# Bias tables from sixteen row copies, read in eighths, and a residual's copy through DRAM issued between weight loads

## The chip, the cores and the metric

The kernel runs on one core of a Trainium2 chip. The metric is the device time of one execution in microseconds (us); a kernel's time is the median of its runs.

## The reference, cut to what matters

A decoder trunk of two layers on 256 tokens of width 1024, all in float32. Each layer adds half a SwiGLU feed-forward, then a mixer, then half a second feed-forward (FFN). Layer 0 mixes with a diagonal state space model (S5); layer 1 with attention whose keys and values are computed once, after layer 0.

```
for layer in range(2):
    h = h + 0.5 * swiglu(rmsnorm(h), w_in (1024 x 5632), w_out (2816 x 1024))
    h = h + mixer(rmsnorm(h))            # layer 0: S5, layer 1: attention
    h = h + 0.5 * swiglu(rmsnorm(h), ...)
    if layer == 0: kv = shared_kv(h)
# attention: logits = q.k * scale + rel_bias[bucket(t - s)], masked where t < s
```

The attention bias depends only on the distance of query and key, for 16 heads: a table of 16 x 256 numbers, which the kernel lays out once as a tile B, with one shifted row per query.

## The kernel before

**Products.** TensorE (PE) has each product in three passes (`mm3`, lines 124 to 126): activations and weights are split into a high and a low half, and high x high, high x low, low x high are added up. Weights come from DRAM as granules of 1 MB (`load_granule`, line 76, issued by SP, two buffers `raw`). ScalarE (ACT) makes the high half, VectorE (DVE) the low half (lines 105 and 108 where a norm's gain is applied, else 92 and 96), half a granule at a time, into five buffers `whi` and five `wlo`.

**An FFN** (`ffn`) goes through 11 chunks of 256 hidden columns. Chunk c first has 48 matmuls of the input product (two granules, tiles `mm`), then SiLU and gate on ACT and DVE (lines 256, 257, tile `g`), then the 24 matmuls of the output product of chunk c-1 (one granule, tiles `o`, in `second`). The transposes of `g` of chunk c-1 on PE (line 211, `transposed`) and their split into the tile `turned` (lines 149 ACT, 150 DVE) stand after the fifth of the chunk's eight k steps. For the last chunk nothing follows: all of `second` of chunk 9, then the four transposes of chunk 10, then `second` of chunk 10, which ends the FFN with the residual added to h (line 235). There are four FFNs; in the second (`w_in2_0`) `perm` is set, and the split of `turned` takes two operations on each engine.

**Work beside the products** is given to `ffn` as a generator `bg`. `background(bg, steps)` is called after each odd k step and at the end of a chunk (once in chunk 0, five times in each later one) and advances the generator; a `yield n` costs n of the calls (a bare `yield` one). What it traces is put behind the last weight split (ACT, DVE) and the last weight load (SP) traced before it.

**The order on each queue** is set when the kernel is built: instructions are taken in traced order, each when the builder's own clock says that what it needs is there, so later loads can go ahead of an earlier copy that is not ready. Each queue then runs in that order on the chip and waits at each instruction for its inputs.

**Around the second FFN.** S5 leaves h with its tokens permuted. Ahead of the FFN, h is written to a DRAM tile `hd` by four copies (line 1019) and read back in natural order by two (line 1021), all issued by SP; `kv_consts` loads small constants; then the FFN runs with `bias_tables` as its background. That multiplies the bias by a one-hot table (line 647, two matmuls), copies the result to `rev` (128 partitions x 384: head h in partition h, repeated eight times), and GpSimd (POOL) issues eight copies `revd<-rev` (line 654), each of 16 partitions, each row sixteen times; then one read `B<-revd` of 2 MB (line 659), 128 partitions. B is first read in the attention, some 410 us later.

Of the kernel before, what the change touches and what calls it, by code (L numbers as in the profile page):

```python
# [9 lines left out]
F32 = mybir.dt.float32  # L10
# [6 lines left out]
P = 128  # L17
D = 1024
# [3 lines left out]
NCH = FF // 256  # L22
# [10 lines left out]
def kernel(ctx: ExitStack, tc: tile.TileContext, A, out):  # L33
    nc = tc.nc
# [9 lines left out]
    dscr = ctx.enter_context(tc.tile_pool(name="dscr", bufs=1, space=bass.MemoryType.DRAM))  # L44
# [4 lines left out]
    def mm_bank():  # L49
        return Banks.mm.tile([P, 512], F32, name="mm")  # L50

    def tr_bank():
        return Banks.tr.tile([P, 512], F32, name=Banks.tag)

    def turn_room():

        return low.tile([P, 2, 1024], F32R, name="turned")


    h = pers.tile([P, 2, D], F32, name="h")  # L60
# [52 lines left out]
    def granules(aps, w=512, gain=None, first=(), eng="av"):  # L113
        for n, ap in enumerate(aps):
            raw = first[n] if n < len(first) else load_granule(ap, w)
            for j in range(2):
                hi, lo = split_half(raw, j, w, gain, ((n % 2) * 2 + j) * 2, eng)
                for s_ in range(2):
                    yield hi[:, s_ * w:(s_ + 1) * w], lo[:, s_ * w:(s_ + 1) * w]
# [77 lines left out]
    def ffn(x, gi, w_in, w_out, res, perm=False, bg=None, steps=1, done=None, first=()):  # L197
        with tc.tile_pool(name="ffn", bufs=2) as fp, tc.tile_pool(name="ps_a", bufs=1, space=PSUM) as pa:
            xT, rs = x.xT, x.rs
            gTs = turn_room()  # L200
            acc2 = [[pa.tile([P, 512], F32, name=f"o{t}{hf}") for hf in range(2)] for t in range(2)]
            g_in = granules([w_in[c, kh] for c in range(NCH) for kh in range(2)], gain=gi, first=first)
            g_out = granules([w_out[j] for j in range(NCH)])

            def transposed(c, g):

                gT = gTs[:, c % 2].rearrange("p (i f c) -> p i f c", i=2, f=2)
                ps = tr_bank()
                for f in range(2):
                    for t in range(2):  # L210
                        T.transpose(ps[:, (f * 2 + t) * P:(f * 2 + t + 1) * P], g[:, t, f * P:(f + 1) * P], ident)  # L211
                if perm:
                    src = ps.rearrange("p (f t e c) -> p f t e c", f=2, t=2, e=2)
                    hi, lo = (gT[:, i].rearrange("p f (c t e) -> p f t e c", t=2, e=2) for i in range(2))
                    for f in range(2):
                        split(hi[:, f], lo[:, f], src[:, f])
                else:
                    split(gT[:, 0], gT[:, 1], ps.rearrange("p (f c) -> p f c", f=2))
                return gT

            def second(c, gT):
                if c < NCH - 1:
                    for f in range(2):
                        for hf in range(2):
                            w = next(g_out)
                            for t in range(2):
                                mm3(acc2[t][hf], gT, f, t, w, c + f == 0, False)
                    return
                ws = [[next(g_out) for _ in range(2)] for _ in range(2)]
                for t in range(2):  # L230
                    for hf in range(2):
                        for f in range(2):
                            mm3(acc2[t][hf], gT, f, t, ws[f][hf], False, f == 1)
                        cs = slice(hf * 512, (hf + 1) * 512)
                        V.scalar_tensor_tensor(out=res[:, t, cs], in0=acc2[t][hf], scalar=0.5, in1=res[:, t, cs], op0=ALU.mult, op1=ALU.add)
                        done(t, hf)

            prev = None
            for c in range(NCH):
                acc = [mm_bank() for _ in range(2)]  # L240
                gT = None
                if c == 0:
                    gemm(acc, xT, g_in, lead=True)
                else:
                    for k in range(KT):
                        w = next(g_in)
                        for t in range(2):
                            mm3(acc[t], xT, k, t, w, k == 0, k == KT - 1)
                        if k == 4:
                            gT = transposed(c - 1, prev)  # L250
                        if k % 2:
                            background(bg, steps)
                g = fp.tile([P, 2, 256], F32, name="g")
                for t in range(2):
                    sl = g[:, t, :]
                    Last.act = S.activation(sl, acc[t][:, 0:256], AF.Silu, scale=rs[:, t:t + 1])  # L256
                    Last.dve = V.scalar_tensor_tensor(out=g[:, t, :], in0=acc[t][:, 256:512], scalar=rs[:, t:t + 1], in1=sl,  # L257
                                                      op0=ALU.mult, op1=ALU.mult)
                if c:
                    second(c - 1, gT)  # L260
                prev = g
                background(bg, steps)
            second(NCH - 1, transposed(NCH - 1, prev))

# [372 lines left out]
    def bias_tables(kp, tp):  # L639

        rb = tp.tile([32, P], F32, name="rb")
        nc.sync.dma_start(out=rb, in_=A["rel_bias"])
        oh = tp.tile([32, 256], F32, name="oh")
        nc.sync.dma_start(out=oh, in_=A["bucket"])
        yield
        ps = tr_bank()
        T.matmul(ps[:, 0:256], lhsT=rb, rhs=oh, start=True, stop=True)
        rev = tp.tile([P, 384], F32, name="rev")
        G.memset(rev[:, 256:384], -1e30)
        V.tensor_copy(rev[:, 0:256], ps[:, 0:256])  # L650
        yield
        dr = dscr.tile([8, 16, 16, 384], F32, name="revd")
        for r in range(8):
            nc.gpsimd.dma_start(out=dr[r].rearrange("q h k -> h q k"), in_=rev[r * 16:(r + 1) * 16].unsqueeze(1).to_broadcast([16, 16, 384]))
            yield
        KV.B = kp.tile([P, 16, 256], F32, name="B")
        a = dr[0]
        src = bass.AP(tensor=a.tensor, offset=a.offset + 127, ap=[[16 * 384 - 1, P], [384, 16], [1, 256]])
        nc.gpsimd.dma_start(out=KV.B, in_=src)
        yield  # L660

    def head_ss(tp, x, nh):

# [15 lines left out]
    def kv_consts(tp):  # L679
        KV.w2 = [tp.tile([P, 64], F32, name=f"cw2{i}") for i in range(2)]  # L680
        KV.kvT = [tp.tile([P, 5, 256], F32, name=f"kvT{i}") for i in range(2)]
        KV.kg = tp.tile([P, 3, 64], F32, name="kg")
        nc.sync.dma_start(out=KV.kg, in_=A["kgain"])
        qg = tp.tile([P, 64], F32, name="qg")
        nc.sync.dma_start(out=qg, in_=A["qgain"])
        G.tensor_tensor(out=KV.kg, in0=KV.kg, in1=qg.unsqueeze(1).to_broadcast([P, 3, 64]), op=ALU.mult)
        for i, x in enumerate("kv"):
            nc.sync.dma_start(out=KV.w2[i], in_=A[f"cmp_{x}_w2"])
            G.memset(KV.kvT[i][:, 4, :], 0.0)
            pos = tp.tile([P, 16], F32, name=f"pos{i}")  # L690
            nc.sync.dma_start(out=pos, in_=A[f"cmp_pos_{x}"])
            G.tensor_copy(KV.kvT[i][:, 4, 0:32:2], pos)

    def shared_kv(x, kp, tp):

# [288 lines left out]
    def fill_next(hc):  # L984
        def done(t, hf):
            if t == 0 and hf == 0:
                acts(hc)
            Nxt.x.fill(t, hf)
        return done
# [24 lines left out]
    with ExitStack() as st:  # L1014
        late = ctx.enter_context(tc.tile_pool(name="late", bufs=1))
        kvp = st.enter_context(tc.tile_pool(name="kvt", bufs=1))
        hd = dscr.tile([256, D], F32, name="hd")
        for i in range(4):
            nc.sync.dma_start(out=hd.rearrange("(c i) d -> i c d", i=4)[i], in_=h[i % 2 * 64:i % 2 * 64 + 64, i // 2, :])
        for t in range(2):  # L1020
            nc.sync.dma_start(out=h[:, t, :], in_=hd[t * P:(t + 1) * P, :])
        kv_consts(kvp)
        ffn(Nxt.x, 1, A["w_in2_0"], A["w_out2_0"], h, perm=True, bg=bias_tables(late, kvp), steps=1, done=fill_next(h))
        x = Nxt.x
        bg = shared_kv(x, late, kvp)
        ffn(x, 3, A["w_in1_1"], A["w_out1_1"], h, bg=bg, steps=1, done=fill_next(h))
# [97 lines left out]
```

## Time and profile before

| what | value |
|---|---|
| time, median of 3 runs | 1056.4 us (1054.69 to 1057.23) |
| the profiled execution: time | 1060.2 us |
| its span | 1058.3 us, mean granted TensorE clock 0.972 |
| busy: PE, weight loads, DVE, ACT, POOL | 94%, 77%, 64%, 55%, 13% |
| moved by DMA | 171.73 MB, 5.24 MB of it written to DRAM |

The profiled execution is 3.8 us above the median of the timed runs and 3.0 us above the slowest of them; 1.9 us of its time lie outside the span. Busy time of PE is modelled from starts, so a busy share near 100% says that matmuls follow one another, not how fast; the start-to-start distance says that.

### The profile page before, as it was taken

The numbers are of one execution on the slowest core, as the hardware profiler recorded it, in microseconds if no ns is written. First come the engines' busy times: TensorE is split into PE (matmuls) and PEld (weight loads), VectorE is DVE, ScalarE is ACT, GpSimd is POOL, SyncE is SP. The second block draws the span as 40 slices with busy tenths as digits, with TensorE's granted clock in tenths as the row PEclk, the third lists the DMA queues.
The fourth block names the chain that finished last, engine by engine and source line by source line (L and its number), as shares of the span: only waits on it lengthen the run. The fifth ranks groups of instructions, "written<-read, shape, count | busy, mean of one in ns | idle before, by whom it ended". The sixth has DMA issues, their size and how long they took to land.

```text
span 1058.3 us, 14566 instructions
## 1 busy us (share of the span) xinstructions
PE 999.4 (94%) x5553; PEld 814.2 (77%) x5553; DVE 672.8 (64%) x1258; ACT 584.7 (55%) x1039; POOL 134.3 (13%) x142
## 2 busy tenths in 40 slices
PE   6999999987798899999999999999987999999998
PEld 5887888785676688887887888887865678888886
DVE  4999854368863566566666456565778866656553
ACT  6577675352263555555755555454876656545452
POOL 3001110327611000000014000000105020000000
PEclk9999999979899899999999999999988899999999
DMA  7556554302358855554554455553312046555551
GB/s 255 197 186 214 194 179 145 120 2 86 116 154 251 281 172 186 199 181 177 183 215 159 160 196 173 188 199 107 100 46 86 30 139 216 173 189 199 187 176 75
DMA packets 27910, 171.73 MB, mean 162 GB/s; under 512 B 4544, under 2 KB 4992, under 8 KB 9024
## 3 DMA queue, kind: packets, MB, share of 16 engines
q1 hardware_dynamic: 26192, 164.77, 45.4%
q0 software_dynamic: 1648, 6.03, 2.2%
q8 instruction: 43, 0.70, 0.3%
q14 instruction: 27, 0.22, 0.1%
HBM read 165.54 MB, written 5.24 MB: 161 GB/s over the span
## 4 chain that ended last, share of the span: by engine, by line
PE 72%; DVE 13%; DMA 5%; ACT 5%; POOL 2%; issue 2%; SPq 0%; ACTq 0%; POOLq 0%; DVEq 0%
PE mm L124 13%; PE mm L125 13%; PE mm L126 13%; PE o L124 7%; PE o L126 7%; PE o L125 7%; DMA raw<-in_w_in_dram 4%; DVE wlo L96 3%; DMA raw<-in_w_out_dram 1%; PE tr L211 1%; DVE wlo L108 1%; DVE Pt L912 1%; ACT whi L92 1%; PE dr L534 1%; DVE w L549 1%
## 5 line engine op out<-in xcount | busy, mean ns | idle before, releaser
L124 PE MATMUL mm<-whi,xT 128*128 128x512 f32 (+2 forms) x800 | 313.4, 392 | 5.9 <-ACT whi L105 2.6
L125 PE MATMUL mm<-wlo,xT 128*128 128x512 f32 (+2 forms) x800 | 306.6, 384 | 0.9 <-DVE wlo L96 0.5
L126 PE MATMUL mm<-whi,xT 128*128 128x512 f32 (+2 forms) x800 | 306.7, 384 | 0.0
L108 DVE SCALAR_TENSOR_TENSOR wlo<-raw,gains,whi 128x512 fp32r<-128x512 f32 (+2 forms) x320 | 221.6, 730 | 111.4 <-ACT whi L105 108.0
L105 ACT ACTIVATE whi<-raw,gains 128x512 fp32r<-128x512 f32 (+2 forms) x320 | 208.2, 696 | 133.2 <-PE mm L126 58.9
L96 DVE TENSOR_TENSOR wlo<-raw,whi 128x1024 fp32r<-128x1024 f32 x140 | 171.1, 1227 | 122.3 <-ACT whi L92 122.2
L92 ACT ACTIVATE whi<-raw 128x1024 fp32r<-128x1024 f32 x148 | 154.7, 1060 | 153.5 <-PE mm L126 58.9
L124 PEld LDWEIGHTS mm<-whi,xT 128*128 128x128 f32 x800 | 151.3, 189 | 36.8 <-ACT whi L105 3.5
L126 PEld LDWEIGHTS mm<-whi,xT 128*128 128x128 f32 x800 | 151.1, 189 | 29.5
L125 PEld LDWEIGHTS mm<-wlo,xT 128*128 128x128 f32 x800 | 151.5, 189 | 28.5 <-DVE wlo L96 1.5
L124 PE MATMUL o<-whi,turned 128*128 128x512 f32 x352 | 139.1, 395 | 8.0 <-ACT turned L149 8.0
L126 PE MATMUL o<-whi,turned 128*128 128x512 f32 x352 | 137.7, 393 | 0.6 <-DVE turned L150 0.6
L125 PE MATMUL o<-wlo,turned 128*128 128x512 f32 x352 | 138.0, 392 | 0.0
L124 PEld LDWEIGHTS o<-whi,turned 128*128 128x128 f32 x352 | 66.7, 190 | 23.4 <-ACT turned L149 10.1
L126 PEld LDWEIGHTS o<-whi,turned 128*128 128x128 f32 x352 | 66.6, 189 | 15.4 <-DVE turned L150 1.4
L125 PEld LDWEIGHTS o<-wlo,turned 128*128 128x128 f32 x352 | 66.7, 189 | 13.6
L256 ACT ACTIVATE g<-mm,rs 128x256 f32<-128x256 f32 x88 | 40.8, 473 | 26.4 <-PE mm L126 26.3
L257 DVE SCALAR_TENSOR_TENSOR g<-mm,rs,g 128x256 f32<-128x256 f32 x88 | 41.8, 481 | 21.3 <-ACT g L256 21.2
L150 DVE TENSOR_TENSOR turned<-tr,turned 128x512 fp32r<-128x512 f32 (+1 forms) x55 | 36.4, 663 | 27.4 <-ACT turned L149 27.0
L149 ACT ACTIVATE turned<-tr 128x512 fp32r<-128x512 f32 (+1 forms) x55 | 33.5, 609 | 33.7 <-PE tr L211 26.7
L146 POOL TENSOR_TENSOR rs<-ms,nhalf 128x1 f32<-128x1 f32 x12 | 6.7, 555 | 229.5 <-DVE ms L145 229.5
L901 ACT ACTIVATE Pt<-Pt,mx 128x128 f32<-128x128 f32 (+1 forms) x64 | 28.4, 445 | 8.9 <-DVE mx L896 8.8
(300 smaller groups left out, 1000.9 us busy)
## 6 DMA issues: line engine op xcount, KB each, us to landing
raw<-in_w_in_dram SPq DMA_DIRECT2D x87, 1024.0 KB, 4.9
raw<-in_w_out_dram SPq DMA_DIRECT2D x44, 1024.0 KB, 4.9
raw<-in_w_kv_dram SPq DMA_DIRECT2D x6, 1024.0 KB, 4.7
raw<-in_w_glu_dram SPq DMA_DIRECT2D x4, 1024.0 KB, 4.8
raw<-in_w_o_dram SPq DMA_DIRECT2D x4, 1024.0 KB, 4.9
revd<-rev POOLq DMA_DIRECT2D x8, 384.0 KB, 15.2
raw<-in_w_qg_dram SPq DMA_DIRECT2D x6, 512.0 KB, 3.6
B<-revd POOLq DMA_DIRECT2D x1, 2048.0 KB, 13.0
```

The source lines that it names most:

```text
L92: Last.act = S.activation(hi, r, AF.Copy)
L96: Last.dve = V.tensor_tensor(out=lo, in0=r, in1=hi.bitcast(F32), op=ALU.subtract)
L105: Last.act = S.activation(hi[:, c], r[:, c], AF.Identity, scale=g_)
L108: i = V.scalar_tensor_tensor(out=lo[:, c], in0=r[:, c], scalar=g_, in1=hi[:, c].bitcast(F32), op0=ALU.mult, op1=ALU.subtract)
L124: T.matmul(ps, lhsT=xh, rhs=wh, start=start, stop=False)
L125: T.matmul(ps, lhsT=xh, rhs=wl, start=False, stop=False)
L126: Last.pe = T.matmul(ps, lhsT=xl, rhs=wh, start=False, stop=stop_)
L149: i = S.activation(dst_hi, src, AF.Copy)
L150: V.tensor_tensor(out=dst_lo, in0=src, in1=dst_hi.bitcast(F32), op=ALU.subtract)
L256: Last.act = S.activation(sl, acc[t][:, 0:256], AF.Silu, scale=rs[:, t:t + 1])
L257: Last.dve = V.scalar_tensor_tensor(out=g[:, t, :], in0=acc[t][:, 256:512], scalar=rs[:, t:t + 1], in1=sl, op0=ALU.mult, op1=ALU.mult)
L901: S.activation(Pt[:, r, br], Pt[:, r, br], AF.Exp, scale=-1.0, bias=mx[:, c:c + 1], accum_out=sm[:, c:c + 1])
```

## The change

Three edits. The eight row copies by POOL, 3.1 MB in DRAM, become two by SP, 0.4 MB: each writes the 128 partitions of `rev` once, which gives 16 copies of the 16 x 384 table. B is read from them by eight DMAs of SP, each for 16 partitions (256 KB), four background calls apart. The copy of h through `hd` is no longer ahead of the FFN but the first part of its background, one DMA at a call, with `kv_consts` behind it and `bias_tables` last. In every FFN the last chunk's transposes and their split move from behind `second` of chunk 9 into its middle, behind its first 12 matmuls.

```diff
-            def second(c, gT):
+            def second(c, gT, fs=(0, 1)):
                 if c < NCH - 1:
-                    for f in range(2):
+                    for f in fs:
...
-                if c:
+                if c == NCH - 1:
+                    second(c - 1, gT, (0,))
+                    last = transposed(c, g)
+                    second(c - 1, gT, (1,))
+                elif c:
                     second(c - 1, gT)
                 prev = g
                 background(bg, steps)
-            second(NCH - 1, transposed(NCH - 1, prev))
+            second(NCH - 1, last)
...
-        dr = dscr.tile([8, 16, 16, 384], F32, name="revd")
+        dr = dscr.tile([16, 16, 384], F32, name="revd")
+        for r in range(2):
+            nc.sync.dma_start(out=dr[8 * r:8 * r + 8].rearrange("q h k -> (q h) k"), in_=rev)
+            yield
+        yield
+        KV.B = kp.tile([P, 16, 256], F32, name="B")
         for r in range(8):
-            nc.gpsimd.dma_start(out=dr[r].rearrange("q h k -> h q k"), in_=rev[r * 16:(r + 1) * 16].unsqueeze(1).to_broadcast([16, 16, 384]))
-            yield
-        KV.B = kp.tile([P, 16, 256], F32, name="B")
-        a = dr[0]
-        src = bass.AP(tensor=a.tensor, offset=a.offset + 127, ap=[[16 * 384 - 1, P], [384, 16], [1, 256]])
-        nc.gpsimd.dma_start(out=KV.B, in_=src)
-        yield
+            src = bass.AP(tensor=dr.tensor, offset=dr.offset + 127 - 16 * r, ap=[[16 * 384 - 1, 16], [384, 16], [1, 256]])
+            nc.sync.dma_start(out=KV.B[16 * r:16 * r + 16], in_=src)
+            yield 4
...
             G.tensor_copy(KV.kvT[i][:, 4, 0:32:2], pos)
+            yield
...
-        hd = dscr.tile([256, D], F32, name="hd")
-        for i in range(4):
-            nc.sync.dma_start(out=hd.rearrange("(c i) d -> i c d", i=4)[i], in_=h[i % 2 * 64:i % 2 * 64 + 64, i // 2, :])
-        for t in range(2):
-            nc.sync.dma_start(out=h[:, t, :], in_=hd[t * P:(t + 1) * P, :])
-        kv_consts(kvp)
-        ffn(Nxt.x, 1, A["w_in2_0"], A["w_out2_0"], h, perm=True, bg=bias_tables(late, kvp), steps=1, done=fill_next(h))
+        def natural_order():
+
+            hd = dscr.tile([256, D], F32, name="hd")
+            for i in range(4):
+                nc.sync.dma_start(out=hd.rearrange("(c i) d -> i c d", i=4)[i], in_=h[i % 2 * 64:i % 2 * 64 + 64, i // 2, :])
+                yield
+            yield
+            for t in range(2):
+                nc.sync.dma_start(out=h[:, t, :], in_=hd[t * P:(t + 1) * P, :])
+                yield 2
+
+        ffn(Nxt.x, 1, A["w_in2_0"], A["w_out2_0"], h, perm=True, bg=chain(natural_order(), kv_consts(kvp), bias_tables(late, kvp)), steps=1, done=fill_next(h))
```

## Rows read from the trace of the kernel before

**Rows 1.** The page: the span in 40 equal slices of 26.5 us: the granted TensorE clock in tenths, and the GB/s moved by DMA. The second FFN lies in slices 11 to 18 (counted from 0).

```profile
PEclk9999999979899899999999999999988899999999
GB/s 255 197 186 214 194 179 145 120 2 86 116 154 251 281 172 186 199 181 177 183 215 159 160 196 173 188 199 107 100 46 86 30 139 216 173 189 199 187 176 75
```

**Rows 2.** The timeline of PE, first part of the second FFN: start (us), duration, line, form, count; in brackets the idle time before it and what ended it. The first row is the first matmul of chunk 1; the matmuls from 352.98 on are those of `second` of chunk 1, the row at 358.19 the thirteenth of its 24.

```profile
314.28 0.50 PE L124 MATMUL mm<-whi,xT 128*128 128x512 f32 x1
319.95 0.69 PE L647 MATMUL tr<-oh,rb 32*128 32x256 f32 x2
322.07 0.60 PE L211 MATMUL tr<-ident,g 128*128 128x128 f32 x4
...
337.26 0.39 PE L126 MATMUL mm<-whi,xT 128*128 128x512 f32 x1
340.30 0.50 PE L124 MATMUL mm<-whi,xT 128*128 128x512 f32 x1 [2.65 <-ACT whi L105]
...
352.98 0.79 PE L124 MATMUL o<-whi,turned 128*128 128x512 f32 x1 [4.39 <-ACT turned L149]
...
358.19 0.40 PE L124 MATMUL o<-whi,turned 128*128 128x512 f32 x1
```

**Rows 3.** The chain that ended last, in order of time, from 313 to 351 us: start, length, what.

```profile
313.18 8.28 DMA raw<-in_w_out_dram
...
324.96 14.48 DMA raw<-in_w_in_dram
...
343.05 7.92 DMA raw<-in_w_in_dram
```

**Rows 4.** Stretches of this stage: from:to, length, busy time of PE, weight loads, DVE, ACT and POOL with counts; then granted clock, DMA share, GB/s.

```profile
322.00:328.00 6.00, 6.00 (x30) 4.97 (x29) 5.43 (x8) 5.80 (x10) 4.30 (x8) 1.00 0.78 95
...
334.00:340.00 6.00, 3.65 (x17) 2.68 (x15) 0.00 (x0) 0.47 (x1) 0.00 (x0) 1.00 1.01 398
...
352.00:358.00 6.00, 5.02 (x12) 3.80 (x13) 5.29 (x10) 4.72 (x9) 0.00 (x0) 0.50 0.98 332
```

**Rows 5.** DMA issues by line: tiles, issuing queue, count, KB each, median us from issue to landing.

```profile
raw<-in_w_in_dram SPq DMA_DIRECT2D x87, 1024.0 KB, 4.9
...
revd<-rev POOLq DMA_DIRECT2D x8, 384.0 KB, 15.2
...
B<-revd POOLq DMA_DIRECT2D x1, 2048.0 KB, 13.0
...
h<-hd SPq DMA_DIRECT2D x2, 512.0 KB, 4.3
cw<-in_cmp_k_w_dram SPq DMA_DIRECT2D x1, 1024.0 KB, 7.1
```

**Rows 6.** The view of the tile `revd`: the spread of that time over its eight copies.

```profile
DMA to landing us min/median/max: 5.9/14.0/20.0
```

**Rows 7.** The timeline of SP, issues only, at the start of the second FFN: start, length to the last issue of the group, line, what, count.

```profile
299.22 0.33 SPq L76 DMA_DIRECT2D raw<-in_w_in_dram  x1
301.02 1.14 SPq L1019 DMA_DIRECT2D hd<-h  x2
...
309.82 1.83 SPq L1021 DMA_DIRECT2D h<-hd  x2
...
313.18 0.36 SPq L76 DMA_DIRECT2D raw<-in_w_out_dram  x1
315.80 9.49 SPq L76 DMA_DIRECT2D raw<-in_w_in_dram  x2
329.47 0.33 SPq L76 DMA_DIRECT2D raw<-in_w_out_dram  x1
```

**Rows 8.** The timeline of POOL: the row copies and the read of B.

```profile
321.75 4.55 POOL L654 DMA_DIRECT2D revd<-rev  x8 [4.88 <-DVE rev L650]
346.25 1.17 POOL L659 DMA_DIRECT2D B<-revd  x1 [19.96 <-DMA revd<-rev]
```

**Rows 9.** The timeline of SP in the fourth FFN, which has no background: the input weights of two chunks that follow one another.

```profile
912.52 5.91 SPq L76 DMA_DIRECT2D raw<-in_w_in_dram  x2
...
929.31 5.92 SPq L76 DMA_DIRECT2D raw<-in_w_in_dram  x2
```

**Rows 10.** The timeline of PE at the end of the fourth FFN: the last but one of the groups of three matmuls of chunk 9, the last transposes, the first and the last group of `second` of chunk 10.

```profile
1045.79 0.39 PE L124 MATMUL o<-whi,turned 128*128 128x512 f32 x1
...
1047.16 0.60 PE L211 MATMUL tr<-ident,g 128*128 128x128 f32 x4
1048.44 0.50 PE L124 MATMUL o<-whi,turned 128*128 128x512 f32 x1 [0.69 <-ACT turned L149]
...
1053.36 0.39 PE L124 MATMUL o<-whi,turned 128*128 128x512 f32 x1
```

**Rows 11.** The timeline of PE and DVE at the ends of the first three FFNs: the first matmul behind the last transposes; for the second FFN also the end of the last gate on DVE.

```profile
208.72 0.50 PE L124 MATMUL o<-whi,turned 128*128 128x512 f32 x1 [0.69 <-ACT turned L149]
...
490.52 0.48 DVE L257 SCALAR_TENSOR_TENSOR g<-mm,rs,g 128x256 f32<-128x256 f32 x1 [0.17 <-ACT g L256]
...
496.79 0.50 PE L124 MATMUL o<-whi,turned 128*128 128x512 f32 x1 [0.94 <-ACT turned L149]
...
733.76 0.50 PE L124 MATMUL o<-whi,turned 128*128 128x512 f32 x1 [1.12 <-ACT turned L149]
```

**Rows 12.** All waits of PE from 520 to 610 us, in the third FFN: line waited for, us in total, times, longest. A load of 1 MB that is no weight, `cw`, was issued by SP between the weights at 526.34 us.

```profile
PE tr L729 <- ACT kvT L735: 1.3, 1, 1.3
```

## The prediction

> **What bounds the kernel now.** I read the page's slices first. The granted clock and the GB/s stand in strange company in slices 12 and 13, the start of the second FFN: the most bytes of any part behind the first slice (251 and 281 GB/s) and a clock of 9 tenths, where the middles of the FFNs have 9 or more at about 190 GB/s [rows 1]. An FFN whose matmuls need no more weights than the others moves more and runs slower; so something else is on the wires.
>
> Then PE's timeline there [rows 2]. The reader is to see two holes: 2.65 us before 340.30, where a high half of an input weight is late, and 4.39 us before 352.98, where the split of `turned` is late because ACT had been held by the weight ahead of it. What they cost is worked out from starts. From 314.28 (first matmul of chunk 1) to 358.19 are 43.9 us. In them lie 48 + 24 + 48 + 12 = 132 matmuls of 512 columns, the bias product and two groups of transposes.
>
> The chain that ended last gives the cause: its pieces in this stretch are not PE but three weight loads, of 8.28, 14.48 and 7.92 us [rows 3]. In the stretches the DMA share is 0.78 at only 95 GB/s, then 1.01 at 398 GB/s [rows 4]: first slow transfers, then full wires. A weight load lands in 4.9 us in the median of all 87 [rows 5]. What was beside the late ones: eight row copies, 14.0 us in the median and 20.0 at worst [rows 6]; on SP's queue the write of h and its read back in front of the weights, the latter at 309.82 [rows 7]; on POOL's the eight copies from 321.75 and the 2 MB read from 346.25 [rows 8]. The 14.48 us load was issued into the eight copies, the 7.92 us one as the last ended and B's read began.
>
> Elsewhere PE sets the pace. In the fourth FFN the weights of one chunk follow those of the last at 929.31 - 912.52 = 16.8 us [rows 9], and six matmuls take 1047.16 - 1045.79 = 1.37 us, so a group of three takes 0.68 [rows 10].
>
> With that pace the lost time of the stage: 132 / 3 x 0.68 = 29.9 us of matmuls, 0.7 for the bias product, 2 x 0.6 for transposes, 31.8 in all [rows 2, 10]. Of 43.9 us 12.1 are lost. [...]
>
> The ends of the FFNs are the second place. Behind the last transposes PE waits for their split: 0.69 us in the first FFN, 0.94 in the second, 1.12 in the third [rows 11], 0.69 in the fourth [rows 10]. In the fourth the last group would start at 1047.16 + 0.60 + 7 x 0.68 = 1052.5; it starts at 1053.36. So 0.84 us are lost, 0.15 more than the hole, since the third pass waits for the low half too.
>
> **The change part by part.** *Row copies.* Eight of 384 KB become two of 192 KB, read from all 128 partitions instead of 16. 3.1 MB become 0.4 MB, and POOL has no DMA left here. By the rows this takes away the slow stretch itself. The two new ones are not in the trace; bounds: nothing, and the fastest old copy, 5.9 us each [rows 6]. They have half its bytes and lie at the fourth chunk, so I take nothing on PE: SP's queue has a cushion, worked out now.
>
> *The cushion.* The output weight was 8.28 - 4.9 = 3.4 us late; only when it was split could the later load be issued, which was 14.48 - 4.9 = 9.6 us late itself [rows 3, 5]. After 13.0 us of lateness PE stood for 2.65. So the halves split ahead cover about 10 us. A second witness: in the third FFN SP issues a whole foreign megabyte, `cw`, between the weights (7.1 us to land [rows 5]), and PE's only wait around it is 1.3 us for another thing [rows 12].
>
> *A new wait on SP.* The first row copy waits for `rev`, so for two matmuls and a copy on DVE; weights stand behind it, and behind those ACT, DVE and PE. On POOL this wait was 4.88 us with no weight behind it [rows 8]. On SP it costs 0 up to 10 us; I take 0. It is late only if the builder's clock runs well ahead of the chip. The eighths wait for the row copies, issued one call and more earlier (a chunk of 16.8 us has five calls, so 3.4 us each [rows 9]).
>
> *B in eighths.* Eight transfers of 256 KB, 13.4 us apart (four calls), in chunks 4 to 9, instead of 2 MB that took 13.0 us [rows 5]. A transfer that writes 16 partitions isn't in the trace; the nearest row is the old copy that reads 16. By bytes, 5.9 us x 256/384 = 3.9 us at the fastest and 20.0 x 256/384 = 13.3 at worst, which was with the others queued before it [rows 6]. In 13.4 us, 2.4 weight loads need 2.4 x 1 MB / 398 GB/s = 6.3 us of the wires [rows 4, 9]. 7.1 us are left; 3.9 fit. Cost nothing, and if the cover is gone, what exceeds 7.1 us a piece.
>
> [...]
>
> *The copy of h.* The four writes need h, so they start at about 301 us as before [rows 7]. The read back moves from 309.82 to behind the first output weight (313.18) and the next input weight (315.80): two of 512 KB, 4.3 us each [rows 5, 7]. Held in full they delay the weights behind them by 8.6 us, under the cushion of 10; as bytes, 2 x 0.5 MB / 398 GB/s = 2.6 us. I take 0. The result is wanted only at the FFN's end, some 180 us on. The small loads of `kv_consts` and the bias inputs move from ahead of the first output weight into chunks 2 and 3; that weight is held by its buffer rather than by them, so nothing.
>
> So all 12.1 us should go. From below: 6, if one hole stays. No more than 12.1, for the pace cannot be beaten.
>
> *Last transposes.* They move behind 12 of the 24 matmuls of chunk 9. The gate must be ready by then: in the second FFN it ends at 490.52 + 0.48 = 491.0; the transposes began at 496.79 - 0.94 - 0.60 = 495.25, so the middle of the products is 4 x 0.68 earlier, at 492.5. The other 12 matmuls take 2.7 us, over twice the longest hole, and hide the split; with `perm` it is two operations in turn on each engine, and ACT may be in a weight, so I keep a remainder. Gain: holes 0.69 + 0.94 + 1.12 + 0.69 = 3.4, and 4 x 0.15 = 0.6; less 0.3 for `perm`: 3.7 us [rows 10, 11]. Bounds: 0, if the builder leaves them where they were, and 4.0. Each end is followed by work that waits for h, so it shows in the time.
>
> *Sum.* 12.1 + 3.7 = 15.8. Against the profiled execution: 1060.2 - 15.8 = 1044.4. That execution is 3.8 us above the median of the timed runs. If the excess lies outside the stage, the timed runs give 1056.4 - 15.8 = 1040.6; if it is in the crowded stage, their gain is smaller by it and they end at 1044.4. I take 1042.
>
> **The rivals.** *One hole comes back on SP.* The read of h or the wait for `rev` eats the cushion. For: both are now between weights. Against: 8.6 us under 10. [...]
>
> *The weights were late for another reason.* Then 12.1 us stay and only the ends gain: 1056.4 - 3.7 = 1052.7, near the 0.3% (3.2 us) below which a measurement of this kernel tells nothing; with the transposes left in place, 1056. For: SP's own copies of h, which stay, were ahead of the late loads. Against: they had landed by about 316, the 14.48 us load was issued at 324.96.
>
> *The eighths are slow* (slower than before). They share SP's queue with the weights. If 16 partitions are served near the worst rate, 12 us a piece, each is 4.9 us over its room: 8 x 4.9 - 10 of cushion = 29 us, less 15.8: 1070. It decides above 7.1 us a piece, and cancels the gain at (15.8 + 10) / 8 + 7.1 = 10.3. Against: the fastest copy, which stood first in its queue, scales to 3.9 us.
>
> **How the numbers follow.** My forecast 0.76, one hole back 0.12, other reason 0.07, slow eighths 0.05. The first two are faster: 0.88; the third I count as the same, 0.07; slower 0.05. The range: from the fastest run before, 1054.7, less 15.8, 1038.9, and 1.9 under it for what two kernels' runs scatter, 1037; up past the one-hole case to 1050. It leaves out the last two cases and the tails.
>
> **What would show it.** After: no wait of PE over 1 us between 314 and 480 us; no weight load above some 9 us in the chain; the clock at 1.0 there; matmuls at 0.68 us a group of three; DRAM written 2.5 MB instead of 5.2; eight B reads of 3 to 5 us; no hole of ACT's `turned` at the ends, `perm` perhaps 0.3. I would be wrong if SP waits for `rev` or `hd` with weights behind it for over 10 us, or if a B read lasts over 7.

## Result, and the profile after

| | before | after |
|---|---|---|
| time, median | 1055.8 us (4 runs, 1054.69 to 1057.23) | 1045.2 us (4 runs, 1044.8 to 1046.92) |
| ratio, 95% interval | | 0.9902 [0.9885, 0.9919] |
| profiled execution: time, span, clock | 1060.2, 1058.3, 0.972 | 1045.5, 1043.4, 0.981 |

The change makes the kernel 10.6 us faster; 14.4 were forecast. Two executions among the runs below, 1863 us in e1 and 2501 us in e4, lie far outside all others and are left out of the medians and ratios. The page after, lines that answer to [rows 1] and to the bytes written (5.24 MB before):

```profile
PEclk9999999989899999999999999999998999999999
GB/s 259 202 192 211 190 181 155 122 2 82 123 125 249 204 212 172 187 168 202 269 175 143 180 171 193 201 172 119 61 81 102 41 121 202 184 182 199 183 182 78
HBM read 165.54 MB, written 2.49 MB: 161 GB/s over the span
```

The 281 GB/s of slice 13 are 204, and its granted clock, 8 tenths in [rows 1] (the prediction reads 9 for both slices), is 9. The three stretches that answer to [rows 4], same columns:

```profile
322.00:328.00 6.00, 6.00 (x28) 4.95 (x28) 3.49 (x6) 2.98 (x5) 0.00 (x0) 1.00 0.80 230
...
334.00:340.00 6.00, 6.00 (x31) 5.00 (x29) 4.66 (x9) 4.26 (x9) 0.00 (x0) 1.00 0.52 178
...
352.00:358.00 6.00, 6.00 (x26) 4.49 (x25) 4.43 (x8) 3.90 (x7) 0.00 (x0) 1.00 0.64 208
```

PE has no gap in them and the clock is 1.00 throughout. All waits of PE from 298 to 375 us, where before had the holes of [rows 2]:

```profile
PE yb L165 <- DVE xT L150: 0.3, 1, 0.3
```

And all its waits from 450 to 520 us:

```profile
PE mm L124 <- ACT whi L105: 2.4, 2, 1.2
PE tr L165 <- DVE h L235: 0.7, 1, 0.7
```

So the old holes are gone, but two of 1.2 us are there that before did not have. PE's timeline shows where, behind the transposes in the middle of two late chunks:

```profile
450.86 0.60 PE L211 MATMUL tr<-ident,g 128*128 128x128 f32 x4
452.64 0.73 PE L124 MATMUL mm<-whi,xT 128*128 128x512 f32 x2 [1.19 <-ACT whi L105]
...
464.04 0.60 PE L211 MATMUL tr<-ident,g 128*128 128x128 f32 x4
465.83 0.73 PE L124 MATMUL mm<-whi,xT 128*128 128x512 f32 x2 [1.19 <-ACT whi L105]
```

ACT's timeline there tells why:

```profile
443.04 2.58 ACT L105 ACTIVATE whi<-raw,gains 128x512 fp32r<-128x512 f32 x4 [2.39 <-DMA raw<-in_w_in_dram]
451.49 0.62 ACT L149 ACTIVATE turned<-tr 128x256 fp32r<-128x256 f32 x1 [5.88 <-PE tr L211]
451.90 1.30 ACT L105 ACTIVATE whi<-raw,gains 128x512 fp32r<-128x512 f32 x2
...
464.68 0.62 ACT L149 ACTIVATE turned<-tr 128x256 fp32r<-128x256 f32 x1 [5.40 <-PE tr L211]
465.09 2.52 ACT L105 ACTIVATE whi<-raw,gains 128x512 fp32r<-128x512 f32 x4
```

ACT stood idle for 5.88 and 5.40 us at the head of its queue, waiting for transposes that were not due yet; the weight halves that PE needed next stood behind. It was not the load: SP had issued it at 440.23, and by the view of that one load it landed after 7.4 us, at 447.6, almost 4 us before ACT came free.

```profile
437.33 0.33 SPq L76 DMA_DIRECT2D raw<-in_w_in_dram  x1
437.71 0.42 SPq L664 DMA_DIRECT2D B<-revd  x1
440.23 0.33 SPq L76 DMA_DIRECT2D raw<-in_w_in_dram  x1
```

```profile
DMA to landing us min/median/max: 7.4/7.4/7.4
```

**What the stage loses**, by a measure that serves all runs: the distance between the first output matmuls of two neighbouring chunks is 16.79 us undisturbed (17.64 for the chunk that holds the bias product and its operands, which I leave out). Before, two distances are longer, 26.37 and 19.30, so 26.37 + 19.30 - 2 x 16.79 = 12.1 us are lost: the prediction's figure, by another way. After, 18.63 and 18.65: 3.7 us. So 12.1 - 3.7 = 8.4 came back.

The first matmul of the second FFN and of the key and value product behind it, before:

```profile
301.25 0.50 PE L124 MATMUL mm<-whi,xT 128*128 128x512 f32 x1 [0.75 <-ACT xT L149]
...
515.40 0.39 PE L124 MATMUL kv<-whi,xT 128*128 128x512 f32 x1
```

and after:

```profile
297.09 0.50 PE L124 MATMUL mm<-whi,xT 128*128 128x512 f32 x1 [0.75 <-ACT xT L149]
...
502.29 0.39 PE L124 MATMUL kv<-whi,xT 128*128 128x512 f32 x1
```

Between them 214.15 us became 205.20, 8.95 less: the 8.4 and some 0.55 at the FFN's end. Ahead of them lie 4.16 us, of which 0.94 are the first FFN's end; the other 3.2 fell in the rest of the first FFN and in the S5 mixer, which the change does not touch. One stretch there, from the last matmul of the first FFN to the first of the second, took 87.2 us before and 85.6 after, and from 83.8 to 87.8 over all fourteen profiled executions. So I take the 3.2 for scatter between executions; the profiled one of before took 1060.2 against a median of 1055.8.

The DMA issues, to set beside [rows 5, 6], and the spread of the eighths' landing in the view of the tile `B`:

```profile
raw<-in_w_in_dram SPq DMA_DIRECT2D x87, 1024.0 KB, 4.9
...
B<-revd SPq DMA_DIRECT2D x8, 256.0 KB, 8.2
...
h<-hd SPq DMA_DIRECT2D x2, 512.0 KB, 6.2
...
revd<-rev SPq DMA_DIRECT2D x2, 192.0 KB, 2.0
```

```profile
DMA to landing us min/median/max: 7.7/8.2/10.9
```

The weights issued from 356 to 450 us, among the eighths, land later than the 4.9 us of the median of all:

```profile
raw<-in_w_in_dram SPq DMA_DIRECT2D x10, 1024.0 KB, 6.0
raw<-in_w_out_dram SPq DMA_DIRECT2D x5, 1024.0 KB, 7.1
```

The last transposes of the first, third and fourth FFN, to set beside [rows 10, 11]:

```profile
203.14 0.60 PE L211 MATMUL tr<-ident,g 128*128 128x128 f32 x4
203.50 0.47 PE L124 MATMUL o<-whi,turned 128*128 128x512 f32 x1
...
716.55 0.60 PE L211 MATMUL tr<-ident,g 128*128 128x128 f32 x4
716.90 0.47 PE L124 MATMUL o<-whi,turned 128*128 128x512 f32 x1
...
1030.59 0.60 PE L211 MATMUL tr<-ident,g 128*128 128x128 f32 x4
1030.94 0.47 PE L124 MATMUL o<-whi,turned 128*128 128x512 f32 x1
```

The next matmul starts 0.36 us behind them with no bracket: none of the four ends waits for `turned` any more (the second, at 479.97 and 480.32, is like them). From the last input matmul of an FFN to its last output matmul the four ends took 12.30, 13.67, 13.78 and 12.33 us before, and take 11.35, 13.24, 12.87 and 11.34 now: 3.3 less in all.

### The profile page after: what moved, and what is told of

It is laid out like the page before. It is cut to its first block, busy times and chain, and to the rows that moved or that the text cites. A ratio compares the mean times of both kernels' runs of the same rounds, so it can differ in the third digit from the quotient of the medians.

```text
span 1043.4 us, 14529 instructions
## 1 busy us (share of the span) xinstructions
PE 989.7 (95%) x5553; PEld 808.1 (77%) x5553; DVE 669.6 (64%) x1258; ACT 581.7 (56%) x1039; POOL 130.3 (12%) x133
## 4 chain that ended last, share of the span: by engine, by line
PE 81%; DVE 10%; ACT 3%; POOL 3%; DMA 2%; issue 1%; SPq 0%; ACTq 0%; POOLq 0%
PE mm L124 16%; PE mm L125 16%; PE mm L126 15%; PE o L126 7%; PE o L124 7%; PE o L125 7%; PE tr L211 2%; DVE wlo L108 2%; DVE Pt L918 1%; DVE w L553 1%; DMA raw<-in_w_out_dram 1%; DVE wlo L96 1%; PE tr L925 1%; POOL hrr L681 1%; POOL z L513 1%
## 5 line engine op out<-in xcount | busy, mean ns | idle before, releaser
L126 PE MATMUL o<-whi,turned 128*128 128x512 f32 x352 | 137.3, 390 | 0.0
L124 PE MATMUL o<-whi,turned 128*128 128x512 f32 x352 | 136.6, 391 | 0.0
```

What stands on the lines that cost most here:

```text
L124: T.matmul(ps, lhsT=xh, rhs=wh, start=start, stop=False)
L126: Last.pe = T.matmul(ps, lhsT=xl, rhs=wh, start=False, stop=stop_)
```

## Experiments

Two theories of the 3.7 us that did not come back. *Wires*: the eighths (8.2 us to land, 16 partitions each) delay weights. *Order*: the queue orders that the builder sets have become worse on ACT; the transfers are harmless. "Loss" is the sum of the longer chunk distances above 16.79 us in the profiled execution. Medians of before were 1055.0 to 1057.0 us in the several comparisons, so the ratio is the column to compare.

| run | edit | loss, us | median, us | ratio, 95% interval |
|---|---|---|---|---|
| (before) | | 12.1 | 1055.8 | 1 |
| (after) | | 3.7 | 1045.2 | 0.9902 [0.9885, 0.9919] |
| e1_transposes | before + last transposes alone | 10.1 | 1056.0 | 0.9985 [0.9968, 1.0001] |
| e2_tables | before + tables alone | 6.9 | 1052.1 | 0.9957 [0.9936, 0.9978] |
| e3_copy | before + copy of h alone | 9.1 | 1054.3 | 0.9982 [0.9964, 1.0000] |
| e4_pinned | after, ACT's order pinned | 0 | 1041.9 | 0.9873 [0.9854, 0.9893] |
| e5_spread | after, eighths to every eighth partition | 3.7 | 1047.3 | 0.9918 [0.9900, 0.9937] |
| e6_pool | after, eighths issued by POOL | 11.2 | 1054.0 | 0.9980 [0.9966, 0.9995] |
| e7_no_transposes | after without the last transposes' move | 3.7 | 1048.8 | 0.9933 [0.9914, 0.9953] |
| e8_close | e4 with eighths one call apart | 3.8 | 1047.2 | 0.9911 [0.9885, 0.9938] |
| e9_pinned_spread | e4 and e5 together | 0 | 1043.0 | 0.9875 [0.9844, 0.9905] |
| e10_tables_pinned | e2 with ACT's order pinned | 5.1 | 1050.8 | 0.9962 [0.9947, 0.9976] |
| e11_before_pinned | before with ACT's order pinned | 11.9 | 1056.0 | 1.0013 [0.9996, 1.0029] |
| e12_pool_spread | e6 and e5 together | 5.7 | 1045.3 | 0.9919 [0.9894, 0.9944] |

**Order against wires: e4, e5, e9.** e4 tells the builder, in the second FFN alone, to put the split of `turned` behind the ACT instruction traced before it:

```diff
                         if k == 4:
-                            gT = transposed(c - 1, prev)
+                            with ExitStack() as st_:
+                                if perm:
+                                    st_.enter_context(tc.issue_after(Last.act.ins))
+                                gT = transposed(c - 1, prev)
```

> The changed kernel, but in the second FFN ACT's split of `turned` is put behind the last weight split traced before it. No DMA moves: the order on ACT's queue differs only in the chunks from the eighth on, where the changed kernel has two holes of PE (1.19 us each, with what follows them 3.7 us lost). Theory 'order': these holes come from ACT waiting at the split of `turned` for transposes, with weight splits queued behind whose granules have landed; they vanish, the time falls by 3 to 4 us, ratio to the kernel before 0.986 to 0.988. Theory 'wires': the eighths make the granules land late; the holes stay, ratio 0.990 like the changed kernel.

All PE waits from 300 to 500 us are gone, every chunk distance is 16.79 (one 17.64, the bias), and the ratio is 0.9873. Its interval and that of the changed kernel overlap a little; the size of the gain is read from the 3.7 us of chunk distance that are gone. ACT's timeline at the same place:

```profile
448.61 1.34 ACT L105 ACTIVATE whi<-raw,gains 128x512 fp32r<-128x512 f32 x2 [1.99 <-DMA raw<-in_w_in_dram]
452.30 0.62 ACT L149 ACTIVATE turned<-tr 128x256 fp32r<-128x256 f32 x1 [2.35 <-PE tr L211]
452.72 1.30 ACT L105 ACTIVATE whi<-raw,gains 128x512 fp32r<-128x512 f32 x2
```

Two weight halves now go ahead of the wait, as soon as their load lands; the wait itself costs nothing. The eighths still land in 7.6 to 10.0 us here, and the weights issued just ahead of them in 5.8 to 9.0, so the transfers are not what cost the 3.7.

e5 leaves the order alone and makes the transfers quicker:

```diff
-            src = bass.AP(tensor=dr.tensor, offset=dr.offset + 127 - 16 * r, ap=[[16 * 384 - 1, 16], [384, 16], [1, 256]])
-            nc.sync.dma_start(out=KV.B[16 * r:16 * r + 16], in_=src)
+            src = bass.AP(tensor=dr.tensor, offset=dr.offset + 127 - r, ap=[[16 * 384 - 8, 16], [384, 16], [1, 256]])
+            nc.sync.dma_start(out=KV.B[r:128:8], in_=src)
```

> The changed kernel, but each eighth fills every eighth partition (r, r+8, ... r+120) instead of 16 neighbours, from the same row copies. Same bytes, same number of runs of 1 KB, same order on every queue. If the partitions that a piece reaches set its speed ('wires'), its time from issue to landing falls from 8.2 us to 6.5 or less and the late weights and PE's two holes shrink: ratio 0.987 to 0.989. Theory 'order': holes and ratio (0.990) stay, whatever the landing does, since it is the queue order that holds ACT.

The landing in the view of `B`, and PE's waits from 300 to 500 us:

```profile
DMA to landing us min/median/max: 5.7/5.8/6.2
```

```profile
PE mm L124 <- ACT whi L105: 2.4, 2, 1.2
PE mm L124 <- ACT xT L149: 0.7, 1, 0.7
PE yb L165 <- DVE xT L150: 0.3, 1, 0.3
```

2.4 us quicker to land, and the same two holes: 3.7 us lost as before. The weights issued just ahead of the pieces gain too, 5.1 to 5.6 us from issue to landing instead of 5.6 to 9.8 in the changed kernel, and that buys nothing either. e9 puts both edits together.

> The changed kernel with both edits: ACT's split of `turned` kept behind what was traced before it in the second FFN, and each of B's eighths written to every eighth partition. Order theory (what was left of the stage's loss is the order on ACT alone): as with the pinned order alone, ratio 0.9865 to 0.988; the eighths land in about 6 us instead of 7.8, and that buys nothing. Wires theory: quicker eighths give a further gain of 0.001 or more over the pinned kernel.

0.9875 beside 0.9873. With the order right, quicker eighths buy nothing. The wires theory of the 3.7 us has fallen.

**Is the order the whole story of before? e11.** The same pin on the kernel before, nothing else.

> The kernel before, with nothing changed but ACT's order: the split of `turned` kept in traced order in the second FFN. Wires theory (the row copies and the 2 MB read make weights late, whatever the order): the holes behind 330 us stay, at least 4 us of PE's waits, ratio 0.996 to 1.001. Order theory of the kernel before (the weights' lateness alone would have been covered, and the order turned it into holes): holes under 2 us, ratio 0.988 to 0.992.

```profile
PE o L124 <- ACT turned L149: 10.0, 2, 9.1
```

That is its first row of waits from 300 to 520 us: the stall stays (11.9 us lost). In the kernel before the weights themselves were late; a better order on ACT does not help.

**Spacing and place of the eighths: e8, e6, e12.** e8 is e4 with `yield 4` behind each eighth made a bare `yield`.

> The pinned kernel (ratio 0.987) with the eighths one background call apart instead of four: 3.4 us, SP has four of them between two weights, then two and two. Cushion theory: each piece holds the wires 3.7 us and 0.6 weight loads take 1.6 us of each 3.4, so each piece is 1.9 us over its room, 8 x 1.9 = 15 us of lateness against a cushion of about 10: a hole of 3 to 7 us with its slow clock behind it, ratio 0.991 to 0.995. If only the order on ACT mattered, no hole and 0.987.

The 3.7 us a piece are an estimate; the changed kernel gives it as 8.2 + 0.4 - 4.9, from the median landings of a piece and of a weight and the 0.4 us between their issues. The eighths are issued within 11 us (359.0 to 370.0), land in 7.6 to 18.9, and cost 3.8 us of chunk distance. The ratio is in the expected range, but the hole of 3 to 7 us is not there: PE waits 0.8 us at most for a weight half, and a part of the 3.8 is a wait for the gate like the one that e10 shows below (0.79 and 0.68 us between starts, from 393.40 on). From 370 to 380 us the DMA share is 1.08 at 183 GB/s. So 2 MB of extra traffic is free here when it is spread over the chunks, and was not when bunched (loss 0 in e4, 3.8 here).

e6 gives the eighths to POOL, with nothing else changed.

```diff
-            nc.sync.dma_start(out=KV.B[16 * r:16 * r + 16], in_=src)
+            nc.gpsimd.dma_start(out=KV.B[16 * r:16 * r + 16], in_=src)
```

> The changed kernel, but the eighths are issued by POOL, so SP's queue has only weights from there on. The builder's order on ACT is then the regular one in all of the second FFN. Theory 'order': the two holes vanish, ratio 0.986 to 0.988. Theory 'wires': 2 MB in the same pieces on the same 16 DMA engines delay the same weights, holes of about the same size stay somewhere between chunk 4 and 9, ratio 0.990.

This missed on the slow side. POOL's queue has nothing in it to hold them apart, so `yield 4` spaces them in traced order only. POOL's timeline, PE's first wait from 300 to 500 us, and the stretches around it:

```profile
359.06 4.55 POOL L664 DMA_DIRECT2D B<-revd  x8 [23.04 <-DMA revd<-rev]
```

```profile
PE o L124 <- ACT turned L149: 9.0, 1, 9.0
```

```profile
360.00:370.00 10.00, 10.00 (x46) 8.28 (x45) 4.43 (x5) 3.47 (x4) 3.61 (x7) 1.00 1.04 167
370.00:380.00 10.00, 4.78 (x24) 3.63 (x21) 0.00 (x0) 0.00 (x0) 0.00 (x0) 0.88 1.02 180
380.00:390.00 10.00, 6.20 (x19) 4.81 (x20) 6.41 (x11) 6.78 (x12) 0.00 (x0) 0.61 0.75 176
```

All eight are out by 363.6; the DMA engines are full (1.04, 1.02) at 167 and 180 GB/s, where before had 1.01 at 398 [rows 4]. This is the kernel before over again (a hole of 9.0, then a granted clock of 0.61), without the row copies' 3.1 MB. The two late holes of the changed kernel, however, are not in it: both distances there are 16.79. e6 changes the issuing queue together with the spacing, and ACT is not pinned; e8, bunched less closely on SP's queue and pinned, loses 3.8. How much of the 11.2 belongs to POOL's queue rather than to the spacing is not shown. Full engines, at least, need not mean many bytes, and e12 asks whether it is the layout, by putting e5's spread into e6.

> The changed kernel with B's eighths issued by POOL, as before bunched into some 10 us, but each written to every eighth partition instead of 16 neighbouring ones. With neighbouring partitions there was one hole of 9.0 us, the DMA share was 1.02 to 1.04 at 167 to 180 GB/s in the 20 us around it, and the eighths landed in 6.9 to 24.6 us. Layout theory (16 neighbouring partitions use the wires badly): the same bytes now flow at 250 GB/s or more in that stretch, the slowest eighth lands in under 15 us, the hole is under 4 us, ratio 0.990 to 0.994. Bunching theory (eight transfers beside the weights are too much in whatever layout): the hole stays at 7 to 9 us, ratio 0.996 to 0.999.

```profile
PE o L124 <- ACT turned L149: 3.4, 1, 3.4
```

```profile
360.00:370.00 10.00, 10.00 (x46) 8.26 (x44) 5.26 (x6) 4.04 (x5) 4.36 (x8) 1.00 1.03 247
370.00:380.00 10.00, 6.50 (x30) 4.79 (x29) 1.95 (x3) 2.02 (x4) 0.00 (x0) 1.00 0.93 261
```

The same bytes, issued as closely, now flow at 247 and 261 GB/s; the slowest eighth lands after 17.3 us instead of 24.6 (under 15 was expected), the hole falls from 9.0 to 3.4 and the loss from 11.2 to 5.7. The two input weights issued beside the pieces landed after 18.8 us in e6 and after 11.7 and 13.1 in e12. Both theories had a part: the layout is worth half, and the other half is bunching or POOL's queue. The weights' bytes are in the rates of both runs, and what one piece takes by itself neither shows, since every eighth stood beside a weight.

**The parts alone: e7, e1, e2, e3, e10.** e7 is the changed kernel with the last transposes where they were.

> The changed kernel without its third edit: the last chunk's transposes stay behind all of `second` of chunk 9. By the prediction's term the ends give 3.7 us back: ratio 0.9902 + 0.0035 = 0.9935 to 0.994, PE waits of 0.7 to 1.1 us for `turned` at each of the four ends. If the ends were hidden anyway (work behind them waits for something else), ratio 0.990 to 0.991.

1048.8 against 1045.2, or 0.9933 - 0.9902 = 0.0031, 3.3 us: the ends are worth what was predicted, 3.7, within the scatter. The waits for `turned` at the four ends are 0.69, 2.12, 1.12 and 0.69; the second is longer than expected and than the 0.94 of before [rows 11], so e7 is a rough measure. e1 adds this edit alone to the kernel before.

> The kernel before with the third edit alone: the last chunk's transposes between the halves of `second` of chunk 9. The ends' term says 3.3 to 3.7 us: ratio 0.9965 to 0.997, and the two holes of the second FFN (2.65 and 4.39 us in the kernel before) stay as they are. If the ends are given back by the work behind them, ratio 0.9985 or more.

0.9985, less than expected, and with an interval up to no gain at all. The stage with the late weights is still in it, with one hole of 8.0 us in place of the two of [rows 2]. In its trace the four ends, measured as above, are 3.4 us shorter than before, as the term says; by its time alone the run is inconclusive.

e3 changes only the copy of h and the constants.

> The kernel before with the copy of h and the constants in the background alone; the eight row copies and the one read of B stay on POOL and come about two chunks later, all at once. If they are the cause, the holes move to about 360 to 400 us and keep their size: ratio 0.997 to 1.003. If the copies of h were the cause, the holes go: ratio 0.990 to 0.993.

As expected, little: 9.1 us are still lost, now two chunks later, with one hole of 6.8. The copies of h were not the main cause; whether they had a share in the other 3.0 is not shown. The hole ends at 380.69, and B's read is issued at 383.56, so this hole stands beside the row copies alone.

e2 changes only the tables.

> The kernel before with new bias tables alone: two row copies and eighths by SP; the copy of h and the constants stay ahead of the FFN. If the old row copies and the one read of B on the wires were the cause of the holes before, these go (no PE wait over 1 us before 400 us) and the ratio is 0.990 to 0.994, less what an order on ACT like that of the changed kernel takes. If SP's own copies of h ahead of the weights were the cause (the rival), the holes stay and the ratio is 0.998 to 1.0. The row copies wait for `rev` on SP here with weights behind them: if that eats the cushion, a hole appears around 325 to 335 us.

0.9957: a miss. The old holes are gone, but 6.9 us are lost elsewhere, in distances of 18.46, 18.50 and 20.30. e10 pins ACT's order in it.

> The kernel before with the new tables, and ACT's split of `turned` kept in traced order in the second FFN. With the tables alone the ratio was 0.9957 and some 7 us of chunk periods were lost later in the FFN. Order theory: these go, ratio 0.989 to 0.991 (the stage's 12 us without the ends). If the 7 us come from something else (the copies of h in front of the FFN): ratio stays at 0.995 to 0.997.

A miss for the order on ACT: three distances of about 18.5 stay (5.1 us in all). PE's timeline in one of them, where the input product ends:

```profile
359.64 0.39 PE L126 MATMUL mm<-whi,xT 128*128 128x512 f32 x1
360.44 0.33 PE L211 MATMUL tr<-ident,g 128*128 128x128 f32 x1 [0.41 <-DVE g L260]
361.12 0.55 PE L211 MATMUL tr<-ident,g 128*128 128x128 f32 x3 [0.35 <-DVE g L260]
361.54 1.20 PE L124 MATMUL o<-whi,turned 128*128 128x512 f32 x4
```

Here the transposes have been put right behind the product whose gate they need, and PE waits for the gate: 0.80 us from 359.64 to 360.44 and 0.68 to 361.12, where consecutive matmuls start 0.23 apart. I read that as the builder's order again, on PE this time; the pin on ACT does not touch it. Pinning the transposes on PE in this kernel was not tried. e2 with its 6.9 and e10 with its 5.1 show that tables alone don't bring the stage's gain in this build.

## Why the prediction came out as it did

**The cause: right.** The row copies and B's single read made the weights late. e11 (late weights with a better order, 11.9 us still lost), e3 (without the copies of h in front, 9.1 lost) and e2 (holes of [rows 2] gone with the tables alone) each leave it standing. How the 12.1 divide between row copies and B's read was not isolated; e3's hole of 6.8 came before the read. That transfers of 16 partitions fill the engines at few bytes, read from 0.78 at 95 GB/s [rows 4], is shown by e6 against e12 for pieces that write 16 neighbouring partitions (shares of 1.04 and 1.02 at 167 and 180 GB/s, against 1.03 and 0.93 at 247 and 261 with every eighth partition). The row copies read 16; from 322 to 328 us they had the engines nearly to themselves: POOL's queue took 76.7% of the engines' time for 0.53 of the 0.57 MB moved.

**The stage, 12.1 us: right as the loss, too large as the gain.** Chunk distances give 12.1 as well, and e4 has all of it back: from the second FFN's first matmul to the key and value product it takes 200.88 us against 214.15, 13.3 less, 12.1 of the stage and some 1.1 of the end. The changed kernel has 8.4. The step that failed is the cost of the eighths, "Cost nothing". The working asked only whether they make weights *land* late beyond the cushion. The weights just ahead of them did land up to 4.9 us late (5.6 to 9.8 us), and the cushion covered it, as e4 shows. It never asked what the builder, with more background work and eight more loads among the weights, would do to the order on ACT, though ACT was already where the larger hole of [rows 2] ended ("because ACT had been held"). That order put `turned` ahead of a weight twice, 1.84 us a time. So "no wait of PE over 1 us between 314 and 480" held up to 450 and failed at 452 and 465. The eighths in SP's queue take part in tipping that order: e5 and e7, which leave them there, have the same two holes, and e6 and e12, which give them to POOL, do not. By what step of the builder is not shown.

**The eighths as transfers: cost right, landing wrong.** Predicted 3 to 5 us to land, measured 8.2, and none under 7.7. By the prediction's own sign, a read of B over 7 us, it would be wrong here; the sign was a bad one, since that time costs nothing by itself (e4). All but the first stand 0.4 us behind a weight load on SP's queue (437.33, 437.71), and the eight land 1.5 to 3.0 us behind their weights. What one piece takes by itself, the 3.9 of the scaling by bytes, no run shows. The room was there: e4 loses nothing with them. With the spacing gone (e8) 3.8 us are lost, in part for late weights, as the cushion argument has it in kind.

**SP's new wait: right.** SP waited 4.7 us for `rev` with a weight behind it, close to POOL's 4.88 [rows 8], and PE had no wait in the next 90 us. h's read back (6.2 us each) cost nothing either.

**The ends: right in the sum.** 3.7 predicted; 3.3 by the traces, and e7's ratio agrees. Single ends differ, and the errors partly cancel: the fourth gave 1.0 where 0.84 was worked out, the second and third 0.4 and 0.9 where the same working has 0.8 and 1.3.

**The sum.** From the profile: 8.4 + 3.3 = 11.7 for the change, and 3.2 of scatter: 14.9 beside the 1060.2 - 1045.5 = 14.7 measured. The prediction left open whether the execution's excess of 3.8 lay outside the stage, and took a middle. By the traces most of it lay outside; then its own sum says 1040.6, and 3.7 us of ACT's order make it 1044.3, beside 1045.2. That 1042 missed by 3.2 us and not by 4.6 is the luck of that middle. The pinned kernel, at 1041.9, is what was forecast for this one.

**The rivals.** One hole coming back on SP: the place was wrong (ACT). No run shows the one-hole case that the range to 1050 takes in; two holes of 1.2 us came back instead, 3.7 us in the chunk distances. The 0.3% (3.2 us) named with the second rival is no run's figure; the four executions of before lie 2.5 us (0.24%) apart. The other two rivals did not happen, but slow eighths were nearer than 0.05 suggested: their place on SP's queue between the weights kept them out, as e6 shows with 1054.0.

## To carry over

A transfer's cost is read from what stands beside it: the same 2 MB cost 11 us bunched on POOL's queue in pieces of 16 neighbouring partitions, 6 bunched there and spread over the partitions, and nothing paced between weight loads with ACT's order right; so pace background transfers by a queue that something else holds back. When background work is added to a kernel whose queues are ordered at build time, read the new order before costing the change at nothing: an in-order engine that waits early for a late input holds what is behind it (ACT stood idle for 5.88 and 5.40 us, with the weight halves that PE needed next behind), and one ordering hint was worth 3 us here. Parts measured alone are hard to add up: 0.15% + 0.43% + 0.18% against 0.98% together is inside their intervals, but in the traces the tables alone and the copy alone still lose 6.9 and 9.1 us, in other places than before.

## What the runs showed of the hardware

- The DMA engines were full at very different rates: 398 GB/s with weights beside the last row copies and 332 with B's 128-partition read beside weights (shares 1.01 and 0.98, the second and third stretch of [rows 4]; B's read was issued between them, at 346.25 [rows 8]), 247 to 261 with pieces of every eighth partition (e12, shares 1.03 and 0.93), 167 to 180 with pieces of 16 neighbouring ones (e6, 1.04 and 1.02).
- Issued right behind a 1 MB weight on the same queue, a 256 KB piece of 16 neighbouring partitions landed after 8.2 us in the median, one of every eighth partition after 5.8 (e5). The weight ahead of it landed after 5.6 to 9.8 us beside the first layout and 5.1 to 5.6 beside the second, against 4.9 in the median of all weights. PE lost nothing by either where the pieces were paced and ACT's order was right (e4, e9).
- In e6, as in [rows 4] (0.50 behind the hole of 4.39 us), the granted clock fell behind a long hole, there one of 9.0 us: 1.00 ahead of it, 0.88 in the stretch that holds it and 0.61 in the next ten microseconds. Behind the 1.2 us holes of the changed kernel it stayed at 1.00 (all stretches from 440 to 470 us).
